# Layer 0's MLP by seven products of blocks, its gated sums added to x by accumulating DMAs, modulation tiles in other places

## The chip, the cores and the metric

The kernel runs on one core of a Trainium2 chip. The metric is device time in microseconds of one execution, as the median of several. The engines are named as in the profile: PE (TensorE) multiplies, PEld loads its weights, DVE (VectorE), ACT (ScalarE) and POOL (GpSimd) work elementwise, SP (SyncE) issues loads; each has a queue of its own that it works off in order.

## The reference

Two layers over 640 tokens (512 latent tokens, 128 context tokens) of width 1024. Each layer mixes tokens by four head groups from one input projection, then runs a squared-ReLU MLP of 4096 hidden columns. The six modulation vectors of a layer (shift, scale and gate, twice) come from a product of a conditioning vector with `w_ada`.

```python
def squared_relu_mlp(h, w1, w2):
    return jnp.square(jax.nn.relu(h @ w1)) @ w2

def modulate(x, g, shift, scale):
    return rmsnorm(x, g) * (1 + scale) + shift

def trunk_layer(x, mod, p, mix_fn):
    shift1, scale1, gate1, shift2, scale2, gate2 = jnp.split(mod, N_MOD, axis=-1)
    y, ctx_state = mix_fn(modulate(x, p['norm1'], shift1, scale1))
    x = x + gate1 * y
    x = x + gate2 * squared_relu_mlp(modulate(x, p['norm2'], shift2, scale2), p['w1'], p['w2'])
    return x, ctx_state
...
    for l in range(DEPTH):
...
        mod_lat = (jax.nn.silu(c) @ w_ada[l] + b_ada[l])[:, None, :]
```

## The kernel before

x lies in SBUF with channels on partitions: 8 blocks of 128 channels by 640 tokens, in float32, worked in halves of 384 and 256 tokens (`HALVES`; the last 128 tokens have other gates, so `REGIONS` cuts the second half in two). Every product of float32 operands is done in three matmuls of a high and a low part (`mm3`, L248 to L250). So each weight unit of 128x1024 is loaded by SP into one of three raw buffers (`rawp`), cast to its high part by ACT (L239) and its low part is formed by DVE (L240).

**Layer 1's MLP** uses `Blocks` and `Pair`. A pair is 256 hidden columns. Pairs 0 and 1 are plain products of h. For pairs 2 to 15, `full(p)` loads the two weight blocks (L1151), forms four sums of weight blocks on DVE (L1166 to L1169) and their high and low parts (L253, L254), and does seven products of half size, 84 matmuls of 320 columns, into the PSUM tiles `qa`, `qb` and the two-bank tile `qcd` (halves c and d). V, W and two rr are formed from them on DVE (L1205 to L1218), relu and squares on ACT, and the low part of u on DVE (L1197). `Blocks.sums` makes the matching sums of h once per layer, from a float32 copy of h, `hf`, which `step` writes.

**Layer 0's MLP** uses `two_plain`: plain products, 96 matmuls per pair (384 and 256 columns), a square on POOL (L1144).

**W2.** In both layers `mlp2(j, u)` multiplies the u of two pairs by four units of W2, and `gate_add` (L428) adds gate times product to x on DVE, in three instructions per block of 128 channels: one of 384 columns and two of 128. j runs from 0 to 7; at j = 7 the next norm follows directly.

**Modulation tiles.** `ada_tile(l, ct)` loads 512 KB of `w_ada` into a raw buffer (`adaw`, from the same three) and reduces it twice on DVE (L174, one for each of the two conditionings) with an accumulator read each. The first reduction's elementwise result goes to `junk`, a two-bank PSUM tile that comes from the same two as `qcd`; the second's goes back into the raw buffer. `ada_steps(n)` is called wherever the next n tiles shall run. Before, all of them run in layer 0: some in the mix, 56 in the MLP, one beside each weight unit.

The order on each engine comes from a scheduler that puts instructions of all engines in one program, by the order in which they are written and by its own estimate of when their inputs are there. PE may thus take another product's matmuls between two of a W2 tile.

Of the kernel before, what the change touches and what calls it, by code (L numbers as in the profile page):

```python
# [10 lines left out]
F32 = mybir.dt.float32  # L11
# [8 lines left out]
KT = 8  # L20
# [36 lines left out]
def step_kernel(ctx, tc, xT, wf, wt, wt3, wo1, wo2, wq, wkvs, wada, wnat, wnat2, vec, rows, fnorm, cvec, cache, kpec,  # L57
# [161 lines left out]
    def ada_stream():  # L219
        for v in range(2, 6):  # L220
            for k in range(KT):
                yield 0, v * KT + k
        for ct in range(48):
            yield 1, ct

    ada_it = ada_stream()

# [113 lines left out]
    class Modulate:  # L341
# [7 lines left out]
        def step(self, half, k):  # L349
            if half == 0:  # L350
                self.h[k] = ta([128, 2, TOK], "h")
            if k == 0:
                self.rb[half] = self.norm.rstd(half)
            b0 = HALVES[half][0]
            t = tmp2([128, 384], "mt")
            for t0, n, g in REGIONS[half]:
                o = t0 - b0
                nc.vector.scalar_tensor_tensor(
                    out=t[:, o:o + n], in0=x[:, k, t0:t0 + n], scalar=gains[self.l][g][self.which][:, k:k + 1],
                    in1=self.rb[half][:, o:o + n], op0=ALU.mult, op1=ALU.mult)  # L360
            for t0, n, g in REGIONS[half]:
                o = t0 - b0
                shift = mods[self.l][g][:, self.sh + k:self.sh + k + 1]
                hh = self.h[k][:, 0, t0:t0 + n]
                nc.scalar.activation(hh, t[:, o:o + n], AF.Identity, bias=shift)
                if self.hf is not None:
# [24 lines left out]
    class Blocks(Modulate):  # L391
# [2 lines left out]

        def keep(self):

            self.hf = [cb.rearrange("p a b -> p (a b)")[:, :2 * TOK].rearrange("p (a b) -> p a b", a=2)]
            self.hf += [tb([128, 2, TOK], "hf", F32) for _ in range(3)]

        def sums(self, s):  # L400
            if s == 0:
# [34 lines left out]
    def layer(l, h, next_norm, nxt):  # L436
# [161 lines left out]
        def fm_tile():  # L598
            u = next_unit()
            out = []  # L600
            for t0, n in HALVES:
# [4 lines left out]
                out.append(ps)  # L606
                if t0 == 0:
                    yield
            if l == 0:
                ada_steps(1)  # L610
            return out

        def run(gen):
# [214 lines left out]
        def out1(m):  # L828
            parts = parts1(next_unit())
            out_tile(m, 0, parts, None)  # L830
            if m < NB:
                yield
                out_tile(m, 1, parts, None)
            if l == 0 and m < 3:
                ada_steps(1)


# [210 lines left out]
                run(back)  # L1048

        def load_up():  # L1050
            up["kv"] = load_unit(wkvs[l, :, 0:512], 512)
            up["q"] = load_unit(wq[l])

# [27 lines left out]


        norm2 = Norm()
        blocks = l == DEPTH - 1
        mod = Blocks(norm2, l, 1)
        uo = [load_unit(wo2[l, i]) for i in range(2)]

# [11 lines left out]
        for m in range(NB, 8):  # L1099
            out2(m, 1, parts1(load_unit(wo1[l, m], 768)) + parts2(m))  # L1100
            while m > NB and done * (7 - NB) < 6 * (m - NB):
                if done == 0 and blocks:
                    mod.keep()
                mod.step(0, K_PAIRS[done])
                done += 1
        mod.step(0, K_PAIRS[6])
        mod.step(0, K_PAIRS[7])
        close_phase()
        if blocks:
            open_phase(f"mlp{l}", me=1)  # L1110

        me = phase.get("me")

        class Pair:

# [1 line left out]

            def __init__(self, p, u=None):
# [3 lines left out]
                self.u = u or [pool(), pool()]  # L1126
                self.r, self.q = [None] * 2, [None] * 2

            def plain(self, us, i, half, tail=None):
# [11 lines left out]
                if blocks:  # L1141
# [19 lines left out]

            def w2(self):
                r1, r2 = self.raw
                s23 = me.tile([128, 2, 512], F32, tag="s", bufs=2, name=nm("s"))
                s14 = me.tile([128, 2, 512], F32, tag="s", bufs=2, name=nm("s"))
# [56 lines left out]
        def full(p):  # L1222
# [3 lines left out]
            x_.w2()  # L1226
            x_.first()
            x_.rest()
            return x_.u

        def two_plain(j):
            get = ta if j % 2 == 0 else tb
            two = [Pair(2 * j + i, [get([128, 2, TOK], "u") for _ in range(2)]) for i in range(2)]
            for i in range(4):
                w = load_unit(wf[l, U_W1 + 4 * j + i])
                for half in range(2):
                    two[i // 2].plain([w, w], i % 2, half)
                if l == 0:
                    ada_steps(2 if j == 1 else 1)
            return two[0].u + two[1].u  # L1240

        def mlp2_tile(ut, u, m, half, nrm):
            t0, n = HALVES[half]
            ps = bank("w2")
            for k in range(4):
                c0 = 256 * k + 128 * (m % 2)
                mm3(ps[:, :n], (u[:, 0, c0:c0 + 128], u[:, 1, c0:c0 + 128]), act(ut, k, t0, n), k == 0, k == 3)
            gate_add(ps, m, half, l, 40, nrm)

        def mlp2(j, ut):  # L1250
            if j < 7:
                for i in range(4):
                    u = load_unit(wf[l, U_W2 + 4 * j + i])
                    for m in (2 * i, 2 * i + 1):
                        for half in range(2):
                            mlp2_tile(ut, u, m, half, None)
                    if l == 0:
# [12 lines left out]
        head = [Pair(p, None if blocks else [ta([128, 2, TOK], "u") for _ in range(2)]) for p in range(2)]  # L1270
        ws = [load_unit(wf[l, U_W1 + i], pool=True) for i in range(4)]
        for half in range(2):
            for i in range(4):
                head[i // 2].plain(ws[2 * (i // 2):2 * (i // 2) + 2], i % 2, half)
                if half == 0 and i == 0:
                    for k in K_PAIRS:
                        mod.step(1, k)
        us = head[0].u + head[1].u
        if blocks:
            for s in range(4):  # L1280
                mod.sums(s)
            mlp2(0, us)
            us = full(2) + full(3)
            for j in range(1, 8):
                if j < 7:
                    nxt_us = full(2 * j + 2)
                mlp2(j, us)
                if j < 7:
                    us = nxt_us + full(2 * j + 3)
            close_phase()  # L1290
            del phase["me"]
        else:
            for j in range(8):
                cur = us
                if j < 7:
                    us = two_plain(j + 1)
                mlp2(j, cur)


    open_phase("mix0", lay=1, pt=3)  # L1300
# [152 lines left out]
```

## Time and profile before

| | us |
|---|---|
| median of 3 runs | 1547.53 |
| lowest, highest run | 1541.55, 1549.54 |
| profiled execution, its own time | 1544.02 |
| its span in the trace | 1542.1 |
| PE busy, share of the span | 1473.7, 96% |
| DVE busy, share | 1131.9, 73% |
| ACT busy, share | 668.9, 43% |
| POOL busy, share | 248.2, 16% |

The span reaches from the first to the last instruction in the trace; some 2 us of the execution's time lie outside it. A busy share is an average over stages. In the trace a matmul's own duration overlaps with the next one's, so the rate of PE is read from the distance of starts, and its waits from the idle time in brackets behind a row.

### The profile page before, as it was taken

To read this page: it belongs to the slowest core of one execution; us is meant where nothing else is said; L and a number is where in the kernel's file an instruction comes from. 1 tells how busy PE (TensorE), PEld (TensorE's weight loads), DVE (VectorE), ACT (ScalarE), POOL (GpSimd) and SP (SyncE) were. 2 spreads that over 40 slices of the span, in tenths; PEclk is the share of its full clock that TensorE was granted. 3 is DMA by queue.
4 is the path that set the end of the run, shared out by engine and by line. 5 is a ranking of instruction groups with operands and counts; after the bars stand their busy time and mean duration, and the time that the engine had idled before them with its cause. 6 is when DMAs were issued, how large, how long until landed. Compare 5 with 4: busy or idle time off the path is not lost.

```text
span 1542.1 us, 25203 instructions
## 1 busy us (share of the span) xinstructions
PE 1473.7 (96%) x9716; PEld 1415.8 (92%) x9716; DVE 1131.9 (73%) x2210; ACT 668.9 (43%) x1400; POOL 248.2 (16%) x245
## 2 busy tenths in 40 slices
PE   6898999989999999999999999998999999999997
PEld 2698988979999999999999989898899999999996
DVE  5988878869978778876458666686886676566655
ACT  3544556745222322232236445675835244324422
POOL 2133103343211210120021110222300000000002
PEclk9899999999999999999999989999999999999999
DMA  8544321333555455444212311011222223123211
GB/s 312 199 136 139 100 66 45 103 94 111 190 164 164 139 151 162 151 142 146 66 48 64 123 43 37 30 49 45 83 69 96 69 83 96 57 81 96 83 55 69
DMA packets 50103, 160.22 MB, mean 104 GB/s; under 512 B 6208, under 2 KB 10304, under 8 KB 49984
## 3 DMA queue, kind: packets, MB, share of 16 engines
q1 hardware_dynamic: 48320, 154.68, 31.4%
q10 hardware_dynamic: 1664, 3.93, 0.7%
q8 instruction: 77, 1.26, 0.3%
q14 instruction: 42, 0.34, 0.1%
HBM read 155.55 MB, written 3.05 MB: 103 GB/s over the span
## 4 chain that ended last, share of the span: by engine, by line
PE 78%; DVE 11%; ACT 4%; issue 2%; POOL 1%; DMA 1%; POOLq 0%; DVEq 0%; ACTq 0%; SPq 0%
PE w L250 13%; PE w L249 13%; PE w L248 13%; PE qcd L248 2%; PE fm L248 2%; PE qcd L250 2%; PE fm L250 2%; PE qcd L249 2%; PE fm L249 2%; PE out L248 2%; PE tm L249 2%; PE tm L248 2%; PE tm L250 2%; PE out L249 2%; PE out L250 2%
## 5 line engine op out<-in xcount | busy, mean ns | idle before, releaser
L248 PE MATMUL w<-u,hl 128*128 128x384 f32 (+1 forms) x1024 | 316.9, 310 | 5.0 <-DVE x L428 2.7
L249 PE MATMUL w<-u,hl 128*128 128x384 f32 (+1 forms) x1024 | 317.0, 310 | 0.7 <-DVE u L1197 0.7
L250 PE MATMUL w<-u,hl 128*128 128x384 f32 (+1 forms) x1024 | 316.9, 310 | 0.4 <-DVE hl L240 0.4
L239 ACT CAST hl<-raw 128x1024 fp32r<-128x1024 f32 (+3 forms) x176 | 170.7, 973 | 267.3 <-PE w L250 155.8
L240 DVE TENSOR_TENSOR hl<-raw,hl 128x1024 fp32r<-128x1024 f32 (+3 forms) x156 | 182.7, 1174 | 36.8 <-ACT hl L239 36.4
L428 DVE SCALAR_TENSOR_TENSOR x<-w,mod,x 128x128 f32<-128x128 f32 (+1 forms) x384 | 154.4, 434 | 66.8 <-PE w L250 65.8
L248 PEld LDWEIGHTS w<-u,hl 128*128 128x128 f32 x1024 | 194.4, 190 | 5.8 <-DVE x L428 2.9
L249 PEld LDWEIGHTS w<-u,hl 128*128 128x128 f32 x1024 | 194.7, 190 | 1.0 <-DVE u L1197 1.0
L250 PEld LDWEIGHTS w<-u,hl 128*128 128x128 f32 x1024 | 194.6, 190 | 0.6 <-DVE hl L240 0.6
L249 PE MATMUL w<-h,hl 128*128 128x384 f32 (+1 forms) x576 | 178.4, 311 | 3.8 <-DVE h L369 3.8
L250 PE MATMUL w<-h,hl 128*128 128x384 f32 (+1 forms) x576 | 178.3, 310 | 0.0
L248 PE MATMUL w<-h,hl 128*128 128x384 f32 (+1 forms) x576 | 177.7, 310 | 0.0
L174 DVE CUSTOM_DVE_ANT_0 junk<-adaw,cb,vec 128x1024 f32<-128x1024 f32 x84 | 112.4, 1338 | 61.1 <-DMA adaw<-in_wada 61.1
L270 POOL TENSOR_TENSOR ss<-ss,sq 128x384 f32<-128x384 f32 (+1 forms) x40 | 37.3, 932 | 502.3 <-ACT sq L269 501.6
L1144 POOL TENSOR_TENSOR rq<-rr 128x384 f32<-128x384 f32 (+1 forms) x64 | 65.1, 1018 | 328.9 <-ACT rr L1139 273.3
L174 DVE CUSTOM_DVE_ANT_0 adaw<-adaw,cb,vec 128x1024 f32<-128x1024 f32 x84 | 116.0, 1381 | 1.3
L249 PEld LDWEIGHTS w<-h,hl 128*128 128x128 f32 x576 | 109.4, 190 | 5.7 <-DVE h L369 5.7
L248 PEld LDWEIGHTS w<-h,hl 128*128 128x128 f32 x576 | 109.6, 190 | 0.0
L250 PEld LDWEIGHTS w<-h,hl 128*128 128x128 f32 x576 | 109.6, 190 | 0.0
L248 PE MATMUL fm<-h,hl 128*128 128x256 f32 (+1 forms) x288 | 93.8, 326 | 2.1 <-DVE u L582 2.1
L249 PE MATMUL fm<-h,hl 128*128 128x256 f32 (+1 forms) x288 | 91.6, 318 | 0.0
L250 PE MATMUL fm<-h,hl 128*128 128x256 f32 (+1 forms) x288 | 91.4, 317 | 0.0
(329 smaller groups left out, 3399.6 us busy)
## 6 DMA issues: line engine op xcount, KB each, us to landing
raw<-in_wf SPq DMA_DIRECT2D x146, 512.0 KB, 3.5
adaw<-in_wada SPq DMA_DIRECT2D x84, 512.0 KB, 3.6
raw<-in_wo SPq DMA_DIRECT2D x24, 384.0 KB, 3.1
adan<-in_wnat SPq DMA_DIRECT2D x12, 512.0 KB, 8.3
raw<-in_wt SPq DMA_DIRECT2D x16, 384.0 KB, 3.2
x<-in_xT ACTq DMA_DIRECT2D x4, 640.0 KB, 7.2
raw<-in_wt SPq DMA_DIRECT2D x8, 288.0 KB, 2.8
raw<-in_wo SPq DMA_DIRECT2D x4, 512.0 KB, 3.7
```

Of the source, the lines that this page charges most:

```text
L174: nc.vector.tensor_tensor_reduce(out=raw if g else junk, in0=raw, in1=cb[:, g, :], op0=ALU.mult, op1=ALU.add, scale=1.0, scalar=vecs[l][:, ...
L239: nc.scalar.copy(hl[:, 0, :n], raw[:, :n])
L240: (nc.gpsimd if pool else nc.vector).tensor_sub(hl[:, 1, :n], raw[:, :n], f(hl[:, 0, :n]))
L248: nc.tensor.matmul(out, lhsT=lhs[0], rhs=rhs[0], start=start, stop=False, skip_group_check=more)
L249: nc.tensor.matmul(out, lhsT=lhs[0], rhs=rhs[1], start=False, stop=False, skip_group_check=more)
L250: nc.tensor.matmul(out, lhsT=lhs[1], rhs=rhs[0], start=False, stop=stop, skip_group_check=more)
L270: (nc.gpsimd if pool else nc.vector).tensor_add(self.s[:, t0:t0 + n], self.s[:, t0:t0 + n], sq[:, :n])
L428: nc.vector.scalar_tensor_tensor(out=x[:, m, t0:t0 + n], in0=ps[:, t0 - b0:t0 - b0 + n], scalar=mods[l][g][:, gate + m:gate + m + 1], in1= ...
L1144: nc.gpsimd.tensor_mul(q, r, r)
```

## The change

Layer 0 takes the same path as layer 1: pairs 0 and 1 plain, 14 pairs by `full`, with `Blocks.sums`. `two_plain` is gone, and so is POOL's square. Three things differ from layer 1.

First, the float32 copy of h for the first four blocks of channels lies in `cb` in layer 1; in layer 0 the modulation tiles still read `cb`, so `keep_rest` takes a tile of the MLP's own pool and rebuilds the first 384 tokens as the sum of h's high and low part, two additions on DVE.

Second, for j below 7 layer 0's gated sum is no longer made by DVE: ACT copies the PSUM tile with the gate as scale into an SBUF tile `go` (three instructions per block of channels, five buffers), and POOL issues a DMA that adds `go` into x, 320 KB each, 56 of them.

Third, the modulation tiles are spread anew. Layer 0's mix has 28 (4 more, in its last output tiles), its MLP 43, layer 1's feature tiles 9. In the MLP an even pair has two tiles behind it, an odd pair one, and `mlp2` one ahead of each of its units (three in all for j from 1 to 6, four for j = 0).

```diff
-        for ct in range(48):
-            yield 1, ct
+        for v in (0, 1, 3, 4, 5, 2):
+            for k in range(KT):
+                yield 1, v * KT + k
...
-            self.hf = [cb.rearrange("p a b -> p (a b)")[:, :2 * TOK].rearrange("p (a b) -> p a b", a=2)]
+            self.hf = [cb.rearrange("p a b -> p (a b)")[:, :2 * TOK].rearrange("p (a b) -> p a b", a=2)
+                       if self.l == DEPTH - 1 else None]
             self.hf += [tb([128, 2, TOK], "hf", F32) for _ in range(3)]
+
+        def keep_rest(self):
+            if self.hf[0] is None:
+                self.hf[0] = phase["me"].tile([128, 2, TOK], F32, tag="s", bufs=2, name=nm("hf"))
+                n = HALVES[0][1]
+                for z in range(2):
+                    nc.vector.tensor_add(self.hf[0][:, z, :n], f(self.h[4 * z][:, 0, :n]), f(self.h[4 * z][:, 1, :n]))
...
-            if l == 0:
-                ada_steps(1)
+            ada_steps(1)
...
-            if l == 0 and m < 3:
+            if l == 0 and m < 7:
                 ada_steps(1)
...
-                if blocks:
-                    nc.scalar.activation(q, r, AF.Square)
-                else:
-                    nc.gpsimd.tensor_mul(q, r, r)
+                nc.scalar.activation(q, r, AF.Square)
...
             x_.rest()
+            if l == 0:
+                ada_steps(1 + (p + 1) % 2)
             return x_.u
...
-            gate_add(ps, m, half, l, 40, nrm)
+            if go is None:
+                gate_add(ps, m, half, l, 40, nrm)
+                return
+            for a, w, g in REGIONS[half]:
+                nc.scalar.activation(go[:, a:a + w], ps[:, a - t0:a - t0 + w], AF.Copy,
+                                     scale=mods[l][g][:, 40 + m:41 + m])
+            if half:
+                nc.gpsimd.dma_start(out=x[:, m, :], in_=go, accum_op=ALU.add)
 
         def mlp2(j, ut):
             if j < 7:
                 for i in range(4):
+                    if l == 0 and (i < 3 or j == 0):
+                        ada_steps(1)
                     u = load_unit(wf[l, U_W2 + 4 * j + i])
                     for m in (2 * i, 2 * i + 1):
+                        go = tp([128, TOK], "go") if l == 0 else None
                         for half in range(2):
-                            mlp2_tile(ut, u, m, half, None)
-                    if l == 0:
-                        ada_steps(1)
+                            mlp2_tile(ut, u, m, half, None, go)
...
-        else:
-            for j in range(8):
-                cur = us
-                if j < 7:
-                    us = two_plain(j + 1)
-                mlp2(j, cur)
+        mlp2(0, us)
+        us = full(2) + full(3)
+        for j in range(1, 8):
+            if j < 7:
+                nxt_us = full(2 * j + 2)
+            mlp2(j, us)
+            if j < 7:
+                us = nxt_us + full(2 * j + 3)
```

How the order moves is seen best at one of the six cycles of layer 0's MLP, the one that ends in mlp2(2). SP's queue before, from the second unit of mlp2(0) on: `adaw` are loads of modulation tiles, `raw` loads of weight units.

```order
L171 DMA adaw_4338<-in_wada 128x1024
L237 DMA raw_4343<-in_wf 128x1024
L171 DMA adaw_4406<-in_wada 128x1024
L237 DMA raw_4411<-in_wf 128x1024
L171 DMA adaw_4474<-in_wada 128x1024
L237 DMA raw_4479<-in_wf 128x1024
L171 DMA adaw_4542<-in_wada 128x1024
```

SP's queue in the changed kernel: the odd pair's two blocks (L1156), a tile, the even pair's two blocks, three tiles, and the first unit of W2 for j = 2 (L238).

```order
L1156 DMA raw_5067<-in_wf 128x1024
L1156 DMA raw_5069<-in_wf 128x1024
L171 DMA adaw_5196<-in_wada 128x1024
L1156 DMA raw_5205<-in_wf 128x1024
L1156 DMA raw_5207<-in_wf 128x1024
L171 DMA adaw_5334<-in_wada 128x1024
L171 DMA adaw_5341<-in_wada 128x1024
L171 DMA adaw_5348<-in_wada 128x1024
L238 DMA raw_5355<-in_wf 128x1024
```

Tiles and weight units alternated; now three tiles stand in a row ahead of W2's first unit.

DVE's queue before, in the two plain pairs ahead of mlp2(1): `hl` is the low part of a weight unit, `u` the low part of a pair's output, `mod` an accumulator read.

```order
L240 TENSOR_TENSOR hl_4769<-raw_4767,hl_4769 128x1024
L1145 TENSOR_TENSOR u_4547<-rq_4582,u_4547 128x384
L174 ISA junk_4904,mod_115<-adaw_4902,cb,vec_93 128x1024
L174 ISA mod_115 128x1
L174 ISA adaw_4902,mod_115<-adaw_4902,cb,vec_93 128x1024
L174 ISA mod_115 128x1
L184 SCALAR_TENSOR_TENSOR gain_120<-mod_115,vec_93 128x1
L184 SCALAR_TENSOR_TENSOR gain_122<-mod_115,vec_93 128x1
L240 TENSOR_TENSOR hl_4841<-raw_4839,hl_4841 128x1024
```

DVE's queue in the changed kernel, from the odd pair's last rr (from its `qcd_5105`) on; `qcd_5243` is the even pair's.

```order
L1222 TENSOR_TENSOR rr_5146<-qcd_5105,V_5118 128x320
L1201 TENSOR_TENSOR u_5066<-rr_5160,u_5066 128x640
L255 TENSOR_TENSOR hl_5224<-raw_5207,hl_5224 128x512
L1209 TENSOR_TENSOR V_5256<-qb_5242,q_842_5240 128x320
L174 ISA junk_5336,mod_115<-adaw_5334,cb,vec_93 128x1024
L174 ISA mod_115 128x1
L1201 TENSOR_TENSOR u_5065<-rr_5146,u_5065 128x640
L1211 TENSOR_TENSOR W_5257<-qcd_5243,V_5256 128x320
L174 ISA adaw_5334,mod_115<-adaw_5334,cb,vec_93 128x1024
L174 ISA mod_115 128x1
```

A tile's two reductions stood together between two weight units; now they lie among the pair's rr, u, V and W.

PE's queue in the changed kernel where mlp2(2) begins: `w_858` is its first tile, `hl_5357` the high part of the first W2 unit. The products of `hl_5224` are c of the even pair, those of `hl_5221` its d.

```order
L249 MATMUL qcd_5243<-h_3642,hl_5224 128x320
L250 MATMUL qcd_5243<-h_3642,hl_5224 128x320
L251 MATMUL qcd_5243<-h_3642,hl_5224 128x320
L249 MATMUL w_858_5361<-u_4641,hl_5357 128x384
L250 MATMUL w_858_5361<-u_4641,hl_5357 128x384
L249 MATMUL qcd_5243<-h_3543,hl_5221 128x320
L250 MATMUL qcd_5243<-h_3543,hl_5221 128x320
```

In the changed kernel two matmuls with the high part of W2's first unit stand ahead of the even pair's last product; the other matmuls of that tile come behind it.

## Rows read from the trace of the kernel before

**Rows 1.** The page: busy time, share, instructions of each engine; the chain's shares.

```profile
PE 1473.7 (96%) x9716; PEld 1415.8 (92%) x9716; DVE 1131.9 (73%) x2210; ACT 668.9 (43%) x1400; POOL 248.2 (16%) x245
...
PE 78%; DVE 11%; ACT 4%; issue 2%; POOL 1%; DMA 1%; POOLq 0%; DVEq 0%; ACTq 0%; SPq 0%
```

**Rows 2.** Windows of both MLPs: window, length, busy time of each engine, clock, DMA share.

```profile
342.60:805.50 462.90, 456.71 (x3093) 454.96 (x3093) 350.94 (x628) 134.82 (x231) 81.41 (x78) 0.99 0.44 137
1089.80:1531.20 441.40, 435.14 (x2926) 429.19 (x2924) 299.71 (x530) 187.12 (x301) 15.89 (x15) 1.00 0.23 74
```

**Rows 3.** Timeline of PE: start, duration, instruction, idle time before it and its releaser.

```profile
415.60 0.45 PE L248 MATMUL w<-u,hl 128*128 128x384 f32 x1 [2.72 <-DVE x L428]
...
1124.80 0.45 PE L248 MATMUL w<-u,hl 128*128 128x384 f32 x1 [1.57 <-ACT hl L239]
...
1504.53 0.96 PE L248 MATMUL w<-u,hl 128*128 128x384 f32 x4 [0.75 <-ACT u L1195]
1506.16 0.44 PE L249 MATMUL w<-u,hl 128*128 128x384 f32 x1 [0.67 <-DVE u L1197]
```

**Rows 4.** Groups of DVE in layer 0's MLP: count, busy us, mean ns, idle before.

```profile
L174 DVE CUSTOM_DVE_ANT_0 adaw<-adaw,cb,vec 128x1024 f32<-128x1024 f32 x56 | 76.4, 1365 | 0.8
L174 DVE CUSTOM_DVE_ANT_0 junk<-adaw,cb,vec 128x1024 f32<-128x1024 f32 x56 | 75.0, 1339 | 60.3 <-DMA adaw<-in_wada 60.3
...
L428 DVE SCALAR_TENSOR_TENSOR x<-w,mod,x 128x384 f32<-128x384 f32 x64 | 39.2, 613 | 14.5 <-PE w L250 14.5
L428 DVE SCALAR_TENSOR_TENSOR x<-w,mod,x 128x128 f32<-128x128 f32 x125 | 37.7, 344 | 6.7 <-PE w L250 6.5
...
L174 DVE DVE_READ_ACCUMULATOR2_ANT mod<- 128x1 f32 x112 | 12.3, 110 | 0.0
```

**Rows 5.** Timeline of DVE in layer 1's MLP, at an odd pair's end.

```profile
1236.01 0.49 DVE L1218 TENSOR_TENSOR rr<-qcd,V 128x320 f32<-128x320 f32 x1 [0.30 <-PE qcd L250]
...
1237.30 0.83 DVE L1197 TENSOR_TENSOR u<-rr,u 128x640 fp32r<-128x640 f32 x1
1238.04 0.48 DVE L1205 TENSOR_TENSOR V<-qb,q 128x320 f32<-128x320 f32 x1
1239.09 0.49 DVE L1207 TENSOR_TENSOR W<-qcd,V 128x320 f32<-128x320 f32 x1 [0.56 <-PE qcd L250]
```

**Rows 6.** DMA issues of the page (size, us to landing); ACT's casts in layer 1's MLP.

```profile
raw<-in_wf SPq DMA_DIRECT2D x146, 512.0 KB, 3.5
adaw<-in_wada SPq DMA_DIRECT2D x84, 512.0 KB, 3.6
...
L239 ACT CAST hl<-raw 128x1024 fp32r<-128x1024 f32 x34 | 35.4, 1043 | 31.0 <-PE qcd L250 29.5 <-DMA raw<-in_wf 1.5
L1195 ACT ACTIVATE u<-rr 128x640 fp32r<-128x640 f32 x28 | 20.7, 740 | 0.6
```

**Rows 7.** Timeline of PE: two matmuls of 320 columns, 43 starts apart.

```profile
1224.84 0.31 PE L250 MATMUL qcd<-t,hl 128*128 128x320 f32 x1
...
1231.14 0.31 PE L248 MATMUL qa<-h,hl 128*128 128x320 f32 x1
```

**Rows 8.** Windows of 2 us behind three waits: length, PE busy, granted clock, DMA.

```profile
416.00:418.00 2.00, 2.00 (x11) 0.75 0.27 33
418.00:420.00 2.00, 2.00 (x11) 0.50 0.84 258
420.00:422.00 2.00, 2.00 (x14) 0.90 0.63 219
1126.00:1128.00 2.00, 1.58 (x8) 0.74 0.24 37
1128.00:1130.00 2.00, 2.00 (x8) 0.50 0.57 225
1130.00:1132.00 2.00, 2.00 (x15) 0.90 0.80 231
1506.00:1508.00 2.00, 1.84 (x10) 1.00 0.04 8
```

More of the change, by code (lines that the diff above doesn't have):

```diff
@@ L365, in step @@
                 nc.scalar.activation(hh, t[:, o:o + n], AF.Identity, bias=shift)
-                if self.hf is not None:
+                if self.hf is not None and self.hf[k % 4] is not None:
                     nc.scalar.activation(self.hf[k % 4][:, k // 4, t0:t0 + n], t[:, o:o + n], AF.Identity,
@@ L1050, in load_up @@
         def load_up():
+            if l == DEPTH - 1:
+                ada_steps(96)
             up["kv"] = load_unit(wkvs[l, :, 0:512], 512)
@@ L1083, in layer @@
         norm2 = Norm()
-        blocks = l == DEPTH - 1
         mod = Blocks(norm2, l, 1)
@@ L1101, in layer @@
             while m > NB and done * (7 - NB) < 6 * (m - NB):
-                if done == 0 and blocks:
+                if done == 0:
                     mod.keep()
@@ L1108, in layer, with __init__ @@
         close_phase()
-        if blocks:
-            open_phase(f"mlp{l}", me=1)
-        me = phase.get("me")
+        open_phase(f"mlp{l}", me=1)
+        me = phase["me"]
         class Pair:
-            def __init__(self, p, u=None):
+            def __init__(self, p):
                 self.p = p
@@ L1125, in __init__ @@
                     else (lambda: tb([128, 2, TOK], "u"))
-                self.u = u or [pool(), pool()]
+                self.u = [pool(), pool()]
                 self.r, self.q = [None] * 2, [None] * 2
@@ L1140, in plain @@
                 nc.scalar.activation(hh, r, AF.Square)
-                if blocks:
-                    nc.scalar.activation(q, r, AF.Square)
-                else:
-                    nc.gpsimd.tensor_mul(q, r, r)
+                nc.scalar.activation(q, r, AF.Square)
                 nc.vector.tensor_sub(ui[:, 1, t0:t0 + n], q, f(hh))
@@ L1163, in w2 @@
                 r1, r2 = self.raw
-                s23 = me.tile([128, 2, 512], F32, tag="s", bufs=2, name=nm("s"))
-                s14 = me.tile([128, 2, 512], F32, tag="s", bufs=2, name=nm("s"))
+                s23, s14 = (me.tile([128, 2, TOK], F32, tag="s", bufs=2, name=nm("s"))[:, :, :512] for _ in range(2))
                 nc.vector.tensor_add(s14[:, 0], r2[:, 0], r2[:, 1])
@@ L1228, in full, with mlp2_tile @@
             x_.rest()
+            if l == 0:
+                ada_steps(1 + (p + 1) % 2)
             return x_.u
[L1231 to L1237, printed above, removed]
-                if l == 0:
-                    ada_steps(2 if j == 1 else 1)
-            return two[0].u + two[1].u
-        def mlp2_tile(ut, u, m, half, nrm):
+        def mlp2_tile(ut, u, m, half, nrm, go=None):
             t0, n = HALVES[half]
@@ L1252, in mlp2 @@
                 for i in range(4):
+                    if l == 0 and (i < 3 or j == 0):
+                        ada_steps(1)
                     u = load_unit(wf[l, U_W2 + 4 * j + i])
                     for m in (2 * i, 2 * i + 1):
+                        go = tp([128, TOK], "go") if l == 0 else None
                         for half in range(2):
-                            mlp2_tile(ut, u, m, half, None)
-                    if l == 0:
-                        ada_steps(1)
+                            mlp2_tile(ut, u, m, half, None, go)
             else:
@@ L1268, in mlp2 @@
                     nxt.step(half, k)
-        head = [Pair(p, None if blocks else [ta([128, 2, TOK], "u") for _ in range(2)]) for p in range(2)]
+        head = [Pair(p) for p in range(2)]
         ws = [load_unit(wf[l, U_W1 + i], pool=True) for i in range(4)]
@@ L1275, in layer @@
                 if half == 0 and i == 0:
+                    mod.keep_rest()
                     for k in K_PAIRS:
@@ L1278, in layer @@
         us = head[0].u + head[1].u
[L1279 to L1284, printed above, removed]
-                if j < 7:
[L1286 to L1291, printed above, removed]
-        else:
-            for j in range(8):
-                cur = us
-                if j < 7:
-                    us = two_plain(j + 1)
-                mlp2(j, cur)
+        for s in range(4):
+            mod.sums(s)
+        mlp2(0, us)
[6 more added lines that the diff above has]
+                us = nxt_us + full(2 * j + 3)
+        close_phase()
+        del phase["me"]
     open_phase("mix0", lay=1, pt=3)
```

## Prediction

> **What bounds the kernel now.** I read the page's shares and its chain of waits first [rows 1]: PE, the matmul engine, is busy 96% of the span and makes 78% of the chain that ended last; DVE has 11% of it, ACT 4%. So time goes down only where PE gets fewer columns to stream, and goes up wherever PE is made to wait. Next I cut the span by stage. The two layers do the same MLP, layer 0 by plain products, layer 1 already by the seven products of blocks, so the trace of before holds the price of both forms [rows 2]: layer 0's MLP runs from its first matmul to the first matmul of layer 1 in 462.9 us, layer 1's in 441.4 us. In both PE is busy all but some 6 us, DVE 351 us and 300 us. The other stages get no fewer matmuls, and I looked there only for what the moved modulation tiles touch.
>
> **The products.** Layer 0 takes over layer 1's form, with the same pairs, sizes and W2 units. If all else were as in layer 1, the gain is the difference of the two stretches, 462.9 - 441.4 = 21.5 us. This is better than counting columns, since each stretch already holds its own starting waits: 2.72 us on DVE's x in layer 0, 1.57 us on ACT's hl, 0.75 and 0.67 us near the end in layer 1 [rows 3].
>
> **What layer 1 does not have** is modulation (ada) tiles inside the MLP: each is a 512 KB load and two reductions on DVE with an accumulator read each, 1.34 + 1.37 + 2 x 0.11 = 2.93 us [rows 4]. Before, 56 of them ran in layer 0's MLP, one beside each weight unit, under PE's cover: DVE had 112 us idle there. After, 43 run there. The 4 more in the last output tiles of layer 0's mix and the 9 in layer 1's feature tiles I cost at nothing: layer 0's feature tiles already carry 9 of them, and PE covers them there; uncovered, one would cost 2.9 us.
>
> DVE's total is no problem: the gated sums leave it, 56 x (0.61 + 2 x 0.34) = 73 us [rows 4], and go to ACT, 56 x about 1.1 us, which has that room (135 us busy of 463 before, [rows 2]). The square on ACT instead of POOL is as layer 1 has it.
>
> **Where the order hurts.** What decides is the place of the tiles. Each cycle j = 1 to 6 runs an odd pair with one tile behind it, an even pair with two, then W2 with one tile ahead of its first unit. In SP's queue these are three tile loads in a row before the first W2 unit's load; in DVE's queue the first of them stands between the even pair's V and the odd pair's u. Raw buffers are three, shared by weights and tiles. The two raw blocks of the even pair and the first tile hold all of them; the second and third tile take over the blocks' buffers, and the first W2 unit the first tile's. So W2's load cannot start before that tile's second reduction has read it. Nor can the reduction come earlier: its scratch is the two-bank PSUM tile which the odd pair's c and d hold until DVE's last rr of that pair has read them.
>
> The chain, from the end of the odd pair's last product (zero), with layer 1's rows as durations: rr starts at 0.2 and V ends at 2.6 [rows 5], the stretch from 1236.01 to 1238.04 + 0.48, in which u and a small split lie between; the tile's first reduction and read to 4.0; u 4.7; W 5.2; second reduction and read 6.6; the load lands 3.5 us later [rows 6], 10.1; ACT's cast of 1.05 us [rows 6] gives 11.1, PE starts at 11.3. Against it PE has 53 matmuls of 320 columns left before its first W2 matmul. Forty-three such starts took 1231.14 - 1224.84 = 6.30 us [rows 7], 0.1465 each, so 7.8 us of cover. PE stands 11.3 - 7.8 = 3.5 us, in each of six cycles, since all have the same rows. Bounds: 2.5 if DVE packs its row to the starts and not the ends, 4.5 if the landing takes a microsecond more beside the accumulating DMAs. I take 3.4, 20.4 us in all.
>
> **The clock after a wait.** PE's 2.72 us wait ending at 415.60 [rows 3] is followed by granted clocks of 0.75, 0.50 and 0.90 in the next three 2-us windows [rows 8], that is the lower of the two levels (1.2 instead of 2.4 GHz) for about 3.4 us, a loss of 2 x (0.25 + 0.50 + 0.10) = 1.7 us. The wait of 1.57 us at 1124.80 is followed by 0.74, 0.50, 0.90, again 1.7 us. After 0.75 and 0.67 us at 1504 the clock stayed 1.00 [rows 3, 8]. The new waits are longer than both that cost clock, so I add 1.7 us to each: 10.2 us. Ends: 0 and 6 x 3.4 = 20. The Trainium skill, TensorE: Matmul & The Clock Gate, in the section on HAM oscillation, says the same of a loop that waits for a load once per tile: every tile starts again at the lower clock. By that the full 10.2 us stand; by the 1504 row alone none would.
>
> **Starts.** Layer 0's stored h for the block sums is rebuilt by two DVE adds of 384 columns, 2 x 0.6 = 1.2 us at the head (nearest row: L428 at 384 columns, [rows 4]; 0 if covered). One tile stands before the first W2 unit's low half on DVE, where layer 1 already waits: +2.9 us, one tile [rows 4] (0 to 3.6). Pairs 2, 3 and 4 run in a row with 2 + 1 + 2 tiles and the same three buffers: one tile's time comes uncovered, about +3 (0 to 5). The turn of layers loads masks and tables later than before, behind the MLP's freed memory: +0.8 (0 to 3, a 512 KB landing being 3.5 us [rows 6]).
>
> **Accumulating DMAs.** 56 transfers of 320 KB into x, issued by POOL. The trace shows no such operation. A 512 KB load lands in 3.5 us [rows 6]; from this side an accumulation takes about 3 us, from the other I allow 10 us, since it reads x as well and its descriptors are made by POOL. Nobody waits for one before j = 7, as long as the five go buffers come back: W2 makes one per 3.5 us, so the point is about 14 us. I cost it at nothing. The page SBUF — State Buffer of the Trainium skill, in its note on DVE blocking DMA, says that descriptors made on GpSimd stall while DVE holds the shared port in its fast two-port modes. No run here shows it. It would add to the rival of that name below, not to my sum.
>
> **Sum.** -21.5 + 1.2 + 2.9 + 3.0 + 20.4 + 10.2 + 0.8 = +17.0 us on the profiled execution's 1544.0, so 1561. That execution is 3.5 us under the median of the runs shown, inside their range of 8; I leave it uncorrected.
>
> **Rivals.** (A) **No half clock.** The waits come as worked out, but the clock holds, as after 1504. 1561 - 10.2 = 1550.8; between 1544 and 1554 with S at 2.5 and the starts at their low ends. For it: only some waits in the trace drop the clock. Against: both longer ones in the MLPs did. (B) **As layer 1.** The tile chain is covered, because PE's rows or the buffers leave more room than I read: 1544 - 21.5 + 1 to 5 us = 1524 to 1528. For it: PE waited for no ada load in layer 0 before, with 56 tiles there; DVE's sum falls. Against: the three loads ahead of W2's first unit stand in the order, and before they alternated one to one with weight units. This is the case on the other side, and it decides at S below about 1 us, where six waits cost less than a third of the gain. (C) **go buffers run dry.** If an accumulation needs over 14 us (starved descriptors), ACT stops before the next copy, PSUM banks stay full and PE waits: at 20 us each five buffers give one per 4 us, 0.5 us more for 48 outputs, +24 us on top: about 1585. Nothing in the trace speaks for it.
>
> **How the numbers follow.** Forecast, waits with the lower clock: 0.45, 1555 to 1570. A: 0.28. B: 0.22. C: 0.05. Half a per cent of the median, 7.7 us, is about what a measurement of this kernel can tell from no change: 1539.8 to 1555.3. Slower takes the forecast but its lowest twentieth, and C: 0.48. Same takes A and that twentieth: 0.30. B is faster: 0.22. The range leaves out C, the top of the forecast and nearly half of B: 1526 to 1570.
>
> **What would show it.** After: layer 0's MLP from first matmul to layer 1's first, 480 us by my sum, 470 by A, 443 to 447 by B; six PE waits of about 3.4 us, 52 to 58 us apart, ending with ACT's hl at W2's first matmul; granted clock 0.50 behind each. ACT waiting for a DMA before a copy into go would be C. Wrong in the first place would be the prediction if W2's first load were issued well ahead of the odd pair's u on DVE.

## The result: slower by about one per cent

The changed kernel took 1568.7 us in the median of four runs (1562.1 to 1570.5), the kernel before 1546.0 us (four runs, 1541.6 to 1549.5): a ratio of 1.0147, 95% interval 1.0107 to 1.0186. A second set of runs beside the experiments below gave 1561.6 against 1544.8 us, 1.0107 (1.0078 to 1.0135). The profiled execution took 1562.1 us with a span of 1560.0, so 17.9 us more span than before. The other three executions took 1568.0 to 1570.5 us at a mean granted clock of 0.970 to 0.971, against 0.976 in the profiled one; no trace of them was kept, so the account below is that of the profiled execution, and why the first set's median lies 7.1 us above the second's stays open.

The page of the changed kernel, parts 1, 5 and 6, in the form of [rows 1, 4, 6]. PE has less to do than before (1464 us instead of 1474), but is busy 94% of the span instead of 96%.

```profile
PE 1464.0 (94%) x9548; PEld 1394.3 (89%) x9548; DVE 1153.3 (74%) x2202; ACT 788.6 (51%) x1642; POOL 240.7 (15%) x237
...
L249 PE MATMUL w<-u,hl 128*128 128x384 f32 (+1 forms) x1024 | 316.6, 311 | 8.9 <-ACT hl L240 7.2
L251 PE MATMUL w<-u,hl 128*128 128x384 f32 (+1 forms) x1024 | 314.0, 310 | 5.7 <-DVE hl L241 5.6
...
L1250 POOL DMA_DIRECT2D x<-go x56 | 49.0, 874 | 365.4 <-ACT go L1247 363.1
...
x<-go POOLq DMA_DIRECT2D x56, 320.0 KB, 4.5
```

Windows of both MLPs of the changed kernel (window, length, busy time and instructions of PE, PEld, DVE, ACT and POOL, granted clock, DMA share, GB/s), as in [rows 2]:

```profile
354.00:822.50 468.50, 443.00 (x2927) 432.63 (x2926) 345.58 (x571) 254.37 (x475) 64.68 (x70) 0.99 0.60 161
1108.50:1548.30 439.80, 433.47 (x2926) 427.73 (x2924) 298.71 (x529) 187.17 (x301) 15.88 (x15) 1.00 0.23 74
```

Layer 0's MLP now has the number of matmuls of layer 1's, and takes 468.5 us: 5.5 more than the plain form before, 28.7 more than layer 1's. It also begins 11.5 us later, at 354.05 instead of 342.56; the mix ahead of it has grown. What follows it has the old length, 737.5 us to the end of the span against 736.6. So the 17.9 us are 11.5 of the mix, 5.5 of layer 0's MLP and 0.9 behind it.

In the MLP the same pattern stands in each of the six cycles: three short waits of PE, the last of them at W2's first matmul. They are 0.25 to 0.70, 0.87 to 0.95 and 0.65 to 0.92 us long. Timeline of PE in the changed kernel (start, duration, instruction, idle time before it and its releaser), for one cycle, and the first W2 matmul of mlp2(1) and mlp2(6):

```profile
468.14 0.44 PE L249 MATMUL w<-u,hl 128*128 128x384 f32 x1 [0.85 <-ACT hl L240]
...
574.27 0.41 PE L249 MATMUL qcd<-t,hl 128*128 128x320 f32 x1 [0.40 <-DVE W L1211]
...
577.24 0.39 PE L249 MATMUL qcd<-h,hl 128*128 128x320 f32 x1 [0.95 <-DVE gain L184]
...
579.89 0.44 PE L249 MATMUL w<-u,hl 128*128 128x384 f32 x1 [0.65 <-ACT hl L240]
...
747.84 0.44 PE L249 MATMUL w<-u,hl 128*128 128x384 f32 x1 [0.92 <-ACT hl L240]
```

From 468.14 to 747.84 are five cycles, 55.94 us each.

DVE, SP's loads and ACT in the same cycle:

```profile
569.65 0.49 DVE L1222 TENSOR_TENSOR rr<-qcd,V 128x320 f32<-128x320 f32 x1 [1.02 <-PE qcd L251]
...
571.40 0.48 DVE L1209 TENSOR_TENSOR V<-qb,q 128x320 f32<-128x320 f32 x1
571.80 1.28 DVE L174 CUSTOM_DVE_ANT_0 junk<-adaw,cb,vec 128x1024 f32<-128x1024 f32 x1
...
573.00 0.82 DVE L1201 TENSOR_TENSOR u<-rr,u 128x640 fp32r<-128x640 f32 x1
573.74 0.48 DVE L1211 TENSOR_TENSOR W<-qcd,V 128x320 f32<-128x320 f32 x1
574.14 1.27 DVE L174 CUSTOM_DVE_ANT_0 adaw<-adaw,cb,vec 128x1024 f32<-128x1024 f32 x1
575.34 0.08 DVE L174 DVE_READ_ACCUMULATOR2_ANT mod<- 128x1 f32 x1
...
575.41 1.29 DVE L174 CUSTOM_DVE_ANT_0 junk<-adaw,cb,vec 128x1024 f32<-128x1024 f32 x1
...
576.61 0.48 DVE L1216 TENSOR_TENSOR rr<-W,qcd 128x320 f32<-128x320 f32 x1
...
575.45 0.33 SPq L238 DMA_DIRECT2D raw<-in_wf  x1
...
578.79 1.05 ACT L240 CAST hl<-raw 128x1024 fp32r<-128x1024 f32 x1 [4.44 <-DMA raw<-in_wf]
```

This is the chain of the prediction, link by link. The first tile's last accumulator read starts at 575.34, the load of W2's first unit is issued at 575.45, lands 3.3 us later, ACT casts from 578.79 on, and PE starts at 579.89. The two waits before that one have the same root: the first tile's first reduction (571.80) stands ahead of the even pair's W, and the second tile's (575.41) ahead of its rr. For the wait of 0.95 us the profile names `gain`, the small step right behind rr in DVE's queue; in other cycles it names rr itself.

### The profile page after: what moved, and what is told of

It is laid out like the page before. It is cut to its first block, busy times and chain, and to the rows that moved or that the text cites. A ratio compares the mean times of both kernels' runs of the same rounds, so it can differ in the third digit from the quotient of the medians.

```text
span 1560.0 us, 25091 instructions
## 1 busy us (share of the span) xinstructions
PE 1464.0 (94%) x9548; PEld 1394.3 (89%) x9548; DVE 1153.3 (74%) x2202; ACT 788.6 (51%) x1642; POOL 240.7 (15%) x237
## 5 line engine op out<-in xcount | busy, mean ns | idle before, releaser
L240 ACT CAST hl<-raw 128x1024 fp32r<-128x1024 f32 (+3 forms) x148 | 141.3, 959 | 129.8 <-DMA raw<-in_wf 47.8
L241 DVE TENSOR_TENSOR hl<-raw,hl 128x1024 fp32r<-128x1024 f32 (+3 forms) x128 | 146.5, 1148 | 45.0 <-ACT hl L240 44.7
L254 ACT CAST hl<-s 128x1024 fp32r<-128x1024 f32 x56 | 58.8, 1049 | 147.3 <-PE w L251 83.7
L438 DVE SCALAR_TENSOR_TENSOR x<-w,mod,x 128x128 f32<-128x128 f32 (+1 forms) x216 | 87.2, 434 | 49.7 <-PE w L251 48.8
L1250 POOL DMA_DIRECT2D x<-go x56 | 49.0, 874 | 365.4 <-ACT go L1247 363.1
L254 ACT CAST hl<-raw 128x1024 fp32r<-128x1024 f32 (+1 forms) x56 | 46.6, 833 | 104.7 <-PE w L251 50.9
L255 DVE TENSOR_TENSOR hl<-raw,hl 128x1024 fp32r<-128x1024 f32 (+1 forms) x56 | 53.5, 956 | 57.3 <-ACT hl L254 56.9
L255 DVE TENSOR_TENSOR hl<-s,hl 128x1024 fp32r<-128x1024 f32 x56 | 68.6, 1225 | 34.5 <-ACT hl L254 34.3
L1247 ACT ACTIVATE go<-w,mod 128x384 f32<-128x384 f32 x168 | 65.1, 437 | 41.9 <-PE w L251 30.4
L250 PE MATMUL tm<-hl,h 128*128 128x384 f32 (+1 forms) x240 | 78.7, 328 | 2.3 <-POOL hl L241 2.3
```

The costliest lines, as they stand in the source:

```text
L240: nc.scalar.copy(hl[:, 0, :n], raw[:, :n])
L241: (nc.gpsimd if pool else nc.vector).tensor_sub(hl[:, 1, :n], raw[:, :n], f(hl[:, 0, :n]))
L250: nc.tensor.matmul(out, lhsT=lhs[0], rhs=rhs[1], start=False, stop=False, skip_group_check=more)
L254: nc.scalar.copy(h_out, src)
L255: nc.vector.tensor_sub(l_out, src, f(h_out))
L438: nc.vector.scalar_tensor_tensor(out=x[:, m, t0:t0 + n], in0=ps[:, t0 - b0:t0 - b0 + n], scalar=mods[l][g][:, gate + m:gate + m + 1], in1= ...
```

## The experiments

Times are medians; a ratio stands against the kernel before on the same chip, with its 95% interval. "MLP" is layer 0's MLP in the profiled execution, from its first matmul to layer 1's first.

| kernel | time, us | ratio, interval | MLP begins | MLP takes |
|---|---|---|---|---|
| before | 1546.0 | | 342.6 | 463.0 |
| changed | 1568.7 | 1.0147 (1.0107 to 1.0186) | 354.1 | 468.5 |
| e1 without 39 tiles | 1540.3 | 0.9979 (0.9965 to 0.9993) | 354.1 | 447.5 |
| e2 four tiles moved in the mix | 1554.5 | 1.0077 (1.0052 to 1.0103) | 345.1 | 467.8 |
| e3 gated sums on DVE | 1561.8 | 1.0119 (1.0091 to 1.0147) | 354.0 | 468.6 |
| e4 accumulation alone | 1540.9 | 0.9975 (0.9957 to 0.9993) | 346.7 | 460.9 |
| e5 W2 first | 1549.7 | 1.0019 (1.0001 to 1.0037) | 350.9 | 450.4 |
| e6 tiles in W2 only | 1555.2 | 1.0063 (1.0042 to 1.0085) | 355.3 | 454.8 |
| e7 32 in the mix, W2 only | 1546.3 | 1.0012 (0.9995 to 1.0030) | 358.2 | 448.0 |
| e8 32 in the mix, odd pairs | 1550.2 | 1.0028 (1.0003 to 1.0053) | 360.1 | 449.1 |
| e9 put together | 1531.3 | 0.9906 (0.9886 to 0.9927) | 345.0 | 443.4 |
| e10 the same, sums on DVE | 1532.2 | 0.9916 (0.9888 to 0.9945) | 345.8 | 446.6 |
| e11 changed, again | 1561.6 | 1.0107 (1.0078 to 1.0135) | 353.2 | 467.5 |

**e1: without the tiles.** Of the 43 tiles of layer 0's MLP only the four in mlp2(0) are left. The other 39 never run, so layer 1's modulation, which this kernel sets to zero at its start, is not the model's; those lines are not in the cut shown.

```diff
             x_.rest()
-            if l == 0:
-                ada_steps(1 + (p + 1) % 2)
             return x_.u
...
-                    if l == 0 and (i < 3 or j == 0):
+                    if l == 0 and j == 0:
                         ada_steps(1)
```

> The changed kernel without 39 of the 43 modulation tiles of layer 0's MLP (the four that layer 0's own last gate needs stay; layer 1's modulation is left at zero, so its result is not the model's). Theory T1, the tiles' loads and reductions stand ahead of W2's first load and among the pair's evacuations: layer 0's MLP falls from 468 us to 443 to 447, the time falls by 21 to 25 us to about 1545. Rival T2, the accumulating DMAs and ACT's copies cost it (contention, ACT late): the MLP stays above 460 and the time above 1560.

The MLP fell to 447.5 us and the time to 1540.3, 28 us under the changed kernel's first runs and 21 under its second ones; the spans differ by 20.9. The first W2 matmuls of its six cycles are not waited for, and stand as far apart as in layer 1:

```profile
459.63 0.34 PE L253 MATMUL w<-u,hl 128*128 128x384 f32 x1
...
725.51 0.34 PE L253 MATMUL w<-u,hl 128*128 128x384 f32 x1
```

(725.51 - 459.63) / 5 = 53.18 us a cycle, 2.76 less than in the changed kernel. The accumulating DMAs and ACT's copies are all still there, so they are not the cause. But 7.8 us over this kernel's own layer 1 (439.7 us) remain, and the MLP still begins at 354.

**e2: four tiles moved within the mix.**

```diff
-            ada_steps(1)
+            ada_steps(2 if l == 0 and fm_n[0] < 4 else 1)
+            fm_n[0] += 1
...
-            if l == 0 and m < 7:
+            if l == 0 and m < 3:
                 ada_steps(1)
```

> The changed kernel with the four added tiles of layer 0's mix taken out of the last output tiles (three there, as before) and put into its feature tiles (13 instead of 9). If the four tiles among the attention's last evacuations make the mix 11.5 us longer, layer 0's MLP begins at 342 to 346 us instead of 354 and the time falls by 8 to 11 us, to about 1559. Rival: the 11.5 us are from the clock's phase or another order of the mix and stay: 352 to 356, no change of the time.

The MLP begins at 345.1 instead of 354.1, and the span falls by 9.5 us. From the last matmul of the feature tiles to the MLP's first are 139.1 us in the changed kernel and 138.9 to 141.6 in all six kernels with its four tiles there, 131.4 in e2 and 129.4 to 131.4 in all seven without them: they cost about 8 us. The feature tiles themselves take 91.7 to 94.0 us in the three kernels with 13 tiles and 90.2 to 93.6 in the eight with nine, so 13 cost nothing that shows. PE and DVE of the changed kernel show how, near the end of the attention. First PE, then DVE:

```profile
321.82 1.16 PE L245 MATMUL pt<-ident,Pm 128*128 128x128 f32 x6 [1.31 <-DVE yt L711]
324.58 2.03 PE L1002 MATMUL pv<-PTm,vm 128*128 128x256 f32 x10 [1.60 <-DVE PTm L255]
...
318.83 2.49 DVE L241 TENSOR_TENSOR hl<-raw,hl 128x1024 fp32r<-128x1024 f32 x2
321.35 0.42 DVE L711 TENSOR_TENSOR yt<-pv,yt 64x256 f32<-64x256 f32 x1
```

PE in e2 at the same two places:

```profile
314.39 0.66 PE L245 MATMUL pt<-ident,Pm 128*128 128x128 f32 x4 [0.47 <-DVE yt L714]
...
316.50 1.43 PE L1005 MATMUL pv<-PTm,vm 128*128 128x256 f32 x10 [0.75 <-DVE PTm L255]
```

and in the kernel before:

```profile
311.40 0.66 PE L244 MATMUL pt<-ident,Pm 128*128 128x128 f32 x4 [0.47 <-DVE yt L702]
...
313.52 1.44 PE L993 MATMUL pv<-PTm,vm 128*128 128x256 f32 x10 [0.75 <-DVE PTm L254]
```

The four tiles ran from 289.9 to 312.8 us. Behind them two low parts of weight units (2.49 us) stand in DVE's queue directly ahead of `yt`, which PE waits for. From 290 us to the MLP's first matmul PE's waits add up to 9.5 us, in e2 to 3.8. In this stretch PE already waits for DVE's small steps in the kernel before, so there is no cover.

**e3 and e4: the accumulating DMAs.** e3 takes them out of the changed kernel; e4 puts them alone into the kernel before.

```diff
-                        go = tp([128, TOK], "go") if l == 0 else None
+                        go = None
```

> The changed kernel with the gated sums of layer 0 back on DVE (no copies by ACT, no accumulating DMAs). T1 (DVE's place in the cycle decides): DVE gets some 9 us more per cycle, 62 in the six cycles, in W2's stretch where four tiles run as well; waits grow, the time rises by 5 to 20 us to 1574 to 1589. T2 (accumulation costs): the time falls by 5 us or more.

> The kernel before with one part of the change alone: layer 0's gated sums by ACT's copies and accumulating DMAs for j below 7. T1: PE hardly waits for DVE there, so no change: 1541 to 1549. T2: slower by over 5 us.

e3's MLP takes the same 468.6 us, though DVE is busy 404 us in it instead of 346:

```profile
354.00:822.60 468.60, 442.48 (x2926) 432.42 (x2925) 404.37 (x739) 194.52 (x307) 15.68 (x14) 0.99 0.38 122
```

In the profiles neither expectation held: 59 us more on DVE cost nothing, and taking the DMAs away won nothing. The median of e3 agrees with that of the changed kernel's second runs (1561.8 and 1561.6) and lies 6.9 us under that of its first; the profiled spans are 1560.4 and 1560.0. So DVE's total does not decide; its place is what e5 tests. In the kernel before the part alone gives 4 us by the median (0.9975, 0.9957 to 0.9993), 2.1 us in the profile's MLP. That these are the sums' own is not shown: in that MLP the granted clock fell twice in the kernel before, for 3.4 us each, a loss of 1.7 us each, and never in e4.

**e5 and e6: where the tiles stand in a cycle.** e5 leaves an odd pair its tile, gives the even pair none, and runs five behind the loads in mlp2(j). e6 has six there and none at any pair (2, 1, 2, 1).

```diff
-                ada_steps(1 + (p + 1) % 2)
+                ada_steps(p % 2)
...
-                    if l == 0 and (i < 3 or j == 0):
+                    if l == 0 and j == 0:
                         ada_steps(1)
                     u = load_unit(wf[l, U_W2 + 4 * j + i])
+                    if l == 0 and j > 0:
+                        ada_steps((1, 2, 2, 0)[i])
```

> The changed kernel with the three tiles ahead of W2's first unit moved behind it: an odd pair keeps its one tile, an even pair has none, and five run inside mlp2(j) behind the loads of its units (1, 2, 2, 0) for j from 1 to 6; two tiles less in the MLP, done at layer 1's start. Theory P (the prediction's chain: the order of the loads and of DVE's rows ahead of W2's first unit makes the waits): the three waits at an even pair's end and W2's first matmul go, layer 0's MLP 468 to 453 to 456 us, the time 12 to 15 us lower, about 1555. Theory B (DVE's budget as a whole, the same number of tiles per cycle): the waits come elsewhere and the MLP stays above 462.

> The changed kernel with no tile at the pairs at all and six inside mlp2(j) behind the loads (2, 1, 2, 1) for j from 1 to 6; three tiles less in the MLP, done at layer 1's start. Theory P: as with the three moved, plus the 1.3 and 0.7 us at W of the first pairs: MLP 450 to 454, time about 1553. Theory B: MLP above 462. If the six tiles overfill DVE or the raw buffers in W2's stretch, W2's units wait on DVE's hl there.

e5 has as many tiles in a cycle as the changed kernel, and its MLP is 18 us shorter. This is below the expected 453 to 456. It decides against a budget of DVE as a whole and for the order ahead of W2. The first W2 matmuls of mlp2(1) and mlp2(6) have no wait:

```profile
455.23 0.34 PE L249 MATMUL w<-u,hl 128*128 128x384 f32 x1
...
723.34 0.34 PE L249 MATMUL w<-u,hl 128*128 128x384 f32 x1
```

(723.34 - 455.23) / 5 = 53.62 us a cycle. e6, with six, is worse than e5, its MLP just over the expected 450 to 454 us: PE waits for ACT's copies into go, once 2.45 us, because ACT, in order, stands behind a cast for the next pair whose load (4.55 us of waiting) or whose sum from DVE (4.18 us) is late.

```profile
540.83 0.44 PE L249 MATMUL w<-u,hl 128*128 128x384 f32 x1 [1.64 <-ACT go L1245]
547.06 0.44 PE L249 MATMUL w<-u,hl 128*128 128x384 f32 x1 [2.45 <-ACT go L1245]
```

Both also lose in layer 1's mix, where the two or three tiles left over run in one go behind the feature tiles: from the last matmul of those to layer 1's MLP are 133.9 and 136.8 us, against 129.0 in the changed kernel.

**e7 and e8: more tiles in the mix.** Both run 17 tiles in layer 0's feature tiles, three in its last output tiles and none in mlp2(0). e7 has seven in mlp2(j) and none at the pairs; e8 six, and one at odd pairs.

```diff
-            ada_steps(1)
+            ada_steps(2 if l == 0 and fm_n[0] < 8 else 1)
+            fm_n[0] += 1
...
                     u = load_unit(wf[l, U_W2 + 4 * j + i])
+                    if l == 0 and j > 0:
+                        ada_steps((2, 2, 2, 1)[i])
```

> A version meant to beat both: the mix of layer 0 takes 32 tiles (17 in its feature tiles, 3 in the last output tiles), mlp2(0) none, the pairs none, mlp2(1) to mlp2(6) seven each behind the loads. Theory P: MLP begins at 345, the 4.66 us wait on the first W2 unit's low half goes with its tile, MLP 443 to 448 us; time 1527 to 1535 (before about 1545). If the mix cannot hide 17 tiles, it begins later than 348; if seven tiles per W2 stretch are too many for DVE, the MLP is above 455.

> As the version before it, but with one tile behind each odd pair and six in mlp2 instead of seven. Theory P: a tile behind an odd pair costs little, within 3 us of the other version. If DVE is full in the pairs' stretch (10.6 us of work in 12.3 without a tile), the odd pairs' W and rr wait again, 0.4 to 2 us for each of seven, and it is 3 to 10 us slower than the other.

The MLPs are as short as expected (448.0, 449.1), and the wait of 4.66 us on the first W2 unit is gone with its tile; one of 2.54 us for ACT's cast stands there instead. But the feature tiles hide 13 tiles, not 17: they take 105.2 and 106.7 us, and the MLP begins at 358 and 360. PE, POOL and DVE of e7 in that stretch:

```profile
179.61 1.46 PE L245 MATMUL pt<-ident,P 128*128 128x128 f32 x4 [4.86 <-POOL P L743]
...
173.81 6.31 POOL L743 TENSOR_SCALAR P<-P,as 128x512 f32<-128x512 f32 x2 [4.02 <-PE fm L251]
...
174.13 1.26 DVE L174 CUSTOM_DVE_ANT_0 junk<-adaw,cb,vec 128x1024 f32<-128x1024 f32 x1
...
177.81 1.27 DVE L174 CUSTOM_DVE_ANT_0 adaw<-adaw,cb,vec 128x1024 f32<-128x1024 f32 x1
```

POOL's same two steps in the kernel before:

```profile
169.31 1.25 POOL L731 TENSOR_SCALAR P<-P,as 128x512 f32<-128x512 f32 x2 [7.13 <-DVE as L730]
```

Two tiles' four reductions run back to back on DVE from 174.13 to 179.08, and POOL's two steps, of which PE needs the result, last 6.31 us instead of 1.25. Between 120 and 256 us PE's waits for POOL are 8.0 us in e7 and 1.4 in e2. So a second tile is paid here through POOL, too; why POOL's steps last so long beside DVE's reductions no run takes apart.

The two versions differ by 1.1 us in the MLP, so the tile at an odd pair is cheap there. Their medians differ by 3.9 us, more than the 3 expected; in the profiles 1.9 us of the difference stand ahead of the MLP and 2.3 in layer 1's mix.

**e9 and e10: put together.** e9 joins e2's mix and e5's cycles, gives mlp2(5) and mlp2(6) the two left-over tiles, and runs those of mlp2(0) behind the loads too. e10 is e9 with the gated sums on DVE.

```diff
                     u = load_unit(wf[l, U_W2 + 4 * j + i])
+                    if l == 0:
+                        ada_steps(1 if j == 0 else (1, 2, 2, j // 5)[i])
```

> A version put together from what the runs showed: four tiles out of layer 0's last output tiles into its feature tiles (13 there), no tile at an even pair, one at an odd pair, five or six inside mlp2(j) behind the loads (1, 2, 2, 0 or 1), and those of mlp2(0) behind its loads too; no tile is left for layer 1's start. If the two costs add up as separate mechanisms: MLP begins at 345 to 347, takes 446 to 450 us, layer 1 as before, so 9 + 3 us under the version with the three tiles moved: 1535 to 1541, 0.3 to 0.7% under the kernel before. Rival: the feature tiles and the later tiles push something else; then 1545 or more.

> The version before this one with layer 0's gated sums back on DVE, no accumulating DMAs. DVE gets about 10 us more in each W2 stretch of 28 us, beside five tiles (12 to 13 us), four low parts (5 us) and the next pairs' preparation: if DVE's place decides there, the MLP is 5 to 15 us longer; if the accumulating DMAs and ACT's copies (PE's waits on ACT's go) cost more than they free, it is 1 to 4 us shorter.

e9 took 1531.3 us, 0.9906 of the kernel before (0.9886 to 0.9927) and better than expected: the MLP takes 443.4 us, 1.5 over its own layer 1 (441.9).

```profile
345.00:788.40 443.40, 435.33 (x2926) 429.21 (x2925) 345.12 (x571) 249.61 (x475) 64.55 (x70) 1.00 0.63 170
```

e10 has 3.2 us more in the MLP, between the two ranges of its expectation, and the same time within the intervals. Even here the accumulating DMAs bring little.

**e11: the changed kernel again**, to have its time beside e9's.

> The changed kernel once more, beside the others on one chip, to have its median on the same footing: 1562 to 1570.

1561.6 us, under the range by less than 1 us.

## Why the prediction held, point by point

The sum was +17.0 us on the profiled execution, and +17.9 came. That they agree is luck, for the parts did not all hold: in the MLP the terms add up to +16.2 us and +5.5 came; in the mix, put at nothing, +11.5 came. The cause in the MLP is as forecast, three tile loads ahead of W2's first unit and their reductions among the pair's rows (e1, e5). The sign that would have refuted it did not come: W2's first load is issued at 575.45, behind the start of the odd pair's u at 573.00.

- **The products, -21.5 us: right within 2 us.** e9's MLP is 19.6 us shorter than the plain one before, with all 43 tiles inside.
- **The head, +1.2: agrees, but its cause is not shown.** From the first matmul to the first of mlp2(0) the changed kernel takes 36.1 us in layer 0 and 35.0 in layer 1. With the same two adds it is 36.1 and 35.8 in e11, 35.1 and 35.8 in e9, so the difference moves by more than its size.
- **The tile ahead of W2's first low half, +2.9: right place, too small.** PE waits 0.79 us for ACT and 4.66 for DVE there, instead of 1.57 and 0.48 in layer 1, and the clock falls during it. e1 has the same tile, and its stretch from there to mlp2(1) is 68.7 us, against 62.9 in its layer 1: 5.8 us.
- **Pairs 2, 3 and 4 in a row, +3.0: too small.** From mlp2(0)'s first matmul to mlp2(1)'s are 78.0 us, 9.3 over e1. But 12 more matmuls lie between the two in the changed kernel (432 against 420), 1.8 us at the 0.148 us of e1's cycles; less these and one cycle's 2.8, 4.8 us are left, inside the stated 0 to 5. PE waits 0.70 us for ACT at 446.01 and 1.30 us for DVE's W at 447.87, and the lower clock follows (0.52 and 0.63 in the windows of 448 to 452, a loss of 1.7 us).
- **Six waits of 3.4 us, 20.4 us: mechanism right, term too large.** It is 2.76 us a cycle, 16.6 in all. In the cycle shown the idle times are 2.00 us together and the cycle is 2.5 us over e1's (55.67 against 53.18): a matmul of 0.31 us overlaps the next, which starts 0.15 us after it, so each wait costs some 0.16 us more than its idle time. The other links were within 0.2 us of their price from [rows 5, 6] (where 0.2 and the 2.5 us of [rows 5] make 2.7 for V's end, not 2.6); the tile was not: its two reductions take 1.28 and 1.27 us there and the accumulator reads overlap them, so a tile takes 2.4 us of DVE and not 2.93. From the odd pair's rr (569.65, put at 0.2) PE's first W2 matmul comes at 10.4, predicted 11.3.
- **The lower clock, 10.2 us: wrong.** The step that failed was to add to each wait the 1.7 us that two waits in the trace of before had been followed by. The granted clock stayed at 1.00 in all six cycles, and in those of e2, e3 and e11, which have the same tiles in the MLP: 24 of 24. The idle time of a cycle comes in three parts with work between, 0.40, 0.95 and 0.65 us in the one shown, and not as one wait. But one wait is no sure sign either. Layer 1's wait of 1.57 us at its first W2 matmul, one of the two that the price was taken from, stands in all 13 traces; a lower clock follows it in five of them and none in eight, the changed kernel's among these. e6's wait of 2.45 us is followed by none, e7's and e8's of 2.54 us are. What decides is not shown. Windows of the changed kernel (window, length, PE busy, granted clock, DMA share, GB/s) around 396.23, behind 447.87, behind a cycle's waits and behind layer 1's wait, which ends at 1143.47:

```profile
394.00:396.00 2.00, 0.00 (x0) 0.50 0.11 43
396.00:398.00 2.00, 1.77 (x5) 0.50 0.25 49
398.00:400.00 2.00, 2.00 (x8) 0.50 0.53 213
...
448.00:450.00 2.00, 2.00 (x8) 0.52 0.78 248
450.00:452.00 2.00, 2.00 (x11) 0.63 0.37 139
...
578.00:580.00 2.00, 1.35 (x10) 1.00 0.43 88
580.00:582.00 2.00, 2.00 (x14) 1.00 0.56 215
...
1145.00:1147.00 2.00, 1.59 (x9) 1.00 0.22 43
1147.00:1149.00 2.00, 2.00 (x17) 1.00 0.54 219
```

  and of e6 behind its wait that ends at 547.06:

```profile
546.00:548.00 2.00, 0.94 (x5) 1.00 0.40 70
548.00:550.00 2.00, 2.00 (x16) 1.00 0.88 263
```

  The rule of the Trainium skill, TensorE: Matmul & The Clock Gate, on HAM oscillation, names a lower clock for every tile of a loop that waits for a load once per tile. The measurement decides: here no cycle showed it.

- **Four tiles in the last output tiles at nothing: wrong, some 8 us.** The cover that I named was that of the feature tiles, and I did not read the stretch where the tiles go. Its rows in the trace of before show PE waiting for DVE there already. Of the 11.5 us, 8.5 stand in this stretch (139.1 us against 130.7). The other 3.0 stand ahead of it: the last matmul of the feature tiles starts at 214.9 instead of 211.9, and between 140 and 152 us the granted clock was 0.57 instead of 0.86. This part is not the tiles': e4, with the mix of before, had 0.57 there and that matmul at 215.6; e5, with the mix of the changed kernel, had 1.00 and 212.0.
- **The accumulating DMAs at nothing: right.** They land in 4.5 us in the median and 8.7 at most, well under the 14 us at which five buffers would run out. By the page SBUF — State Buffer of the Trainium skill, in its note on DVE blocking DMA, descriptors made on GpSimd stall while DVE holds the shared port in its fast two-port modes. No run here shows whether any did; PE did not pay for it, since e3 without these DMAs has the same MLP. What can make PE wait is ACT's copy behind a cast whose input is late (e6).
- **The turn of layers, +0.8: right**, 0.9 for all behind the MLP.

The MLP took 468.5 us, where the sum gave 480 and rival A, no half clock, 470: A describes it, and its total fell short only for the mix. Rival B, as layer 1, is what e9 shows to be there once the order lets it.

## What to carry to other kernels

Where weights and another stream share a few load buffers, read the load queue in order: the first load of the next stage starts only when the buffer it inherits is free, and a burst of the other stream ahead of it is paid as far as the bounding engine has no other work left to cover it, whatever the mean loads. Put such side work behind the first load of the longest stretch that needs little from that engine, and price a place by the idle time of that very stretch, not of one like it. A form that is quicker on the bounding engine can lose all of its gain to the side work that was spread for the old form; spread that anew, and measure it by cycle length, between points with the same number of matmuls. And compare a forecast with its result stage by stage: here a total within 1 us hid two errors of over 10 us.

## What was not expected of the hardware

A custom DVE reduction of 128x1024 took 1.27 to 1.29 us in the pairs' stretch, against 1.34 and 1.37 us on average in [rows 4]. 320 KB accumulated into SBUF from SBUF landed in 4.5 us in the median (3.6 to 8.7; 6.3 in the median in e9), and POOL was busy 0.87 us with each. The kernel before, in which DVE had 112 us to spare in that MLP, gained a little from handing 67 us of sums to ACT and to DMAs (0.9975); in the changed kernel no gain shows in the profile. The same wait of 1.57 us was followed by a lower clock in five traces of 13. And two steps of POOL that take 1.25 us in the kernel before took 6.31 us in e7, beside four of DVE's reductions in a row.
